# Four weight units behind three FFNs multiply the unnormalised sum and are corrected afterwards

## The chip, the cores and the metric

The kernel runs on one core of a Trainium2 chip. The metric is the time of one execution on the device in microseconds; the median of three runs is shown. Engines are named as in the profile: PE is TensorE (matmuls; PEld its weight loads), DVE is VectorE, ACT is ScalarE, POOL is GpSimd, SP issues most transfers.

## What is computed

The input is 256 tokens of 1024 features in fp32. A first block (a conformer convolution module and a convolutional FFN) is followed by a second block of two layers. Each layer is FFN, mixer, FFN, and a layer norm ends each of the three:

```python
for i in range(2):
    x = layer_norm(ALPHA * x + 0.5 * swiglu(x, gate1[i], up1[i], down1[i]), ln_g[i, 0], ln_b[i, 0])
    proj = x @ w_in[i]                     # i = 0: RWKV-7 mixer, i = 1: stick-breaking attention
    heads = concat([mix(proj), memory_attention(mq, mem_k, mem_v)])
    x = layer_norm(ALPHA * x + heads @ w_out[i], ln_g[i, 1], ln_b[i, 1])
    x = layer_norm(ALPHA * x + 0.5 * swiglu(x, gate2[i], up2[i], down2[i]), ln_g[i, 2], ln_b[i, 2])
```

`layer_norm(y)` is `(y - mean) / sqrt(var + eps) * g + b` over the features of a token. A product of its result with a weight column w is therefore `r * (g*y @ w) - r*mean * (g @ w) + (b @ w)`, with r the reciprocal deviation of the token.

## The kernel before

Activations lie features on partitions: eight tiles of 128 features by 256 tokens. All products are made of three fp32r products: a weight is split into a rounded high part (ScalarE, L226) and the rest (VectorE, L235), an activation likewise (`xh`, `xl`, together `xx`; `split_act`, L499). Weights come as a stream of units of 128 x 1024; `Stream.take` (L243) hands out the next one and splits four units ahead, `split_hi` and `split_lo` (L218, L229) do one part of one unit. A unit of an up-projection is one tile of 128 outputs: eight blocks (one for each input tile) of three matmuls of 256 columns, or two where the wide form (`mm_wide`, L367) moves high and low part in one matmul of 512 columns.

The program is issued in the order of the Python code; each engine runs its own instructions in that order, and waits by semaphores. So what stands earlier in the code on an engine's queue must be finished before what stands later.

`ffn` (L656): 22 pairs of gate and up tiles (`wide_gate`, L714), four banks of PSUM at a time, then the down-projection, eight output tiles of 22 blocks each. Behind each output tile stand the residual (`on_tile`, L1098), its square on ScalarE and a running sum on GpSimd. The layer norm behind it is `Norm.finish` (L1208): short matmuls against a column of 1/1024 give mean and mean square, `keep_warm` (L339) issues 12 matmuls whose result nobody reads, ScalarE and VectorE make the reciprocal deviation, four transposes broadcast deviation and shift into the bank `bc`, and six more unread matmuls follow. `ln_out` (L546) then scales and shifts the tiles group by group (one, one, two, two, two): two VectorE operations that read `bc`, ScalarE's gain and bias into `xh`, VectorE's gain and bias into `xr`, and VectorE's difference into `xl`.

Next come the first four units: `gemm_wides` (L404) in an FFN, `gemm_outs` (L392) in the mixers, both block by block of the input over all four units, so that block k needs only tile k of `xx`. In the RWKV mixer these four are the inputs of the low-rank projections and the memory queries (`project`, L1437); `shifted` (L1427) mixes a tile with the one of the token before, on ScalarE and then VectorE; two transfers of low-rank weights are issued by ScalarE. In stick-breaking they are the memory queries and the first pair of queries and keys (L1963 to L1968).

From there a planner, `weave` (L1297), interleaves generators while the program is built. Each `yield pe, dve, more` says how much time of TensorE and VectorE a step is taken to need and how much later the task may go on; a task whose time has not come is passed over, and lower priorities go first. It fixes an order once; at run time nothing is reordered. The tasks that matter here:

```python
def lora(self, lora, dwa):        # RWKV, priority 3
    yield 0.0, 0.0, 3.0
    ...                           # products of lora weights with dwa, two per step
def attention(self):              # stick-breaking, priority 1
    yield 0.0, 0.0, 1.2
    ...                           # scores of pair p from queries and keys
```

The main task (priority 5) makes the remaining units through `gemm_out_parts` (L377), which yields 0.66 after every second block.

## Time and profile before

| | us |
|---|---|
| median of three runs (lowest, highest) | 1495.84 (1494.53, 1499.8) |
| the profiled execution | 1493.3 |
| its span | 1491.5 |
| PE busy | 1435.5 (96%) |
| DVE busy | 1064.8 (71%) |
| ACT busy | 843.4 (57%) |
| POOL busy | 109.2 (7%) |

The table's busy times are sums over the span, and matmuls overlap each other in the record: the starts of two neighbours lie closer together than one of them lasts. So the starts are what tells TensorE's pace. Times in the text count from the span's start. The chain of waits follows the work that ended last back from the end; a row of the timeline gives start, duration, engine, line, operation, output and inputs, and in brackets how long the engine had been idle before and what ended that.

### The profile page before, as it was taken

To read this page: it belongs to the slowest core of one execution; us is meant where nothing else is said; L and a number is where in the kernel's file an instruction comes from. 1 tells how busy PE (TensorE), PEld (TensorE's weight loads), DVE (VectorE), ACT (ScalarE), POOL (GpSimd) and SP (SyncE) were. 2 spreads that over 40 slices of the span, in tenths; PEclk is the share of its full clock that TensorE was granted. 3 is DMA by queue.
4 is the path that set the end of the run, shared out by engine and by line. 5 is a ranking of instruction groups with operands and counts; after the bars stand their busy time and mean duration, and the time that the engine had idled before them with its cause. 6 is when DMAs were issued, how large, how long until landed. Compare 5 with 4: busy or idle time off the path is not lost.

```text
span 1491.5 us, 26146 instructions
## 1 busy us (share of the span) xinstructions
PE 1435.5 (96%) x10737; PEld 1288.1 (86%) x10737; DVE 1064.8 (71%) x1677; ACT 843.4 (57%) x1479; POOL 109.2 (7%) x96
## 2 busy tenths in 40 slices
PE   8888899999999999999999999999999999999997
PEld 7868799998888888898888888888888988888886
DVE  7897788884877657888568776587765655687753
ACT  6796466685565536651346655365553566465542
POOL 1110100000000010040010000100001011100010
PEclk9998899999999999999989999999999999999998
DMA  9775445565355553230034555535555322265540
GB/s 381 285 253 187 155 170 194 186 228 198 147 194 196 188 188 125 92 136 4 3 112 176 192 198 185 183 139 200 183 184 198 127 109 103 99 225 195 198 169 29
DMA packets 39145, 250.38 MB, mean 168 GB/s; under 512 B 4337, under 2 KB 4849, under 8 KB 12274
## 3 DMA queue, kind: packets, MB, share of 16 engines
q1 hardware_dynamic: 38594, 247.60, 45.5%
q8 instruction: 84, 1.38, 0.4%
q10 hardware_dynamic: 432, 1.11, 0.2%
q14 instruction: 35, 0.29, 0.1%
HBM read 247.65 MB, written 1.05 MB: 167 GB/s over the span
## 4 chain that ended last, share of the span: by engine, by line
PE 82%; DVE 11%; ACT 5%; issue 2%; POOL 0%; DVEq 0%; ACTq 0%; POOLq 0%
PE acc L370 26%; PE acc L358 15%; PE gu L358 7%; PE gu L370 7%; PE gu L363 4%; PE gu L364 4%; PE r L1737 2%; PE acc L412 2%; DVE wlo L235 2%; PE st L1219 1%; DVE mraw L595 1%; ACT whi L226 1%; PE gu L346 1%; DVE ys L555 1%; PE acc L862 1%
## 5 line engine op out<-in xcount | busy, mean ns | idle before, releaser
L235 DVE TENSOR_TENSOR wlo<-wraw,whi 128x1024 fp32r<-128x1024 f32 x416 | 522.4, 1266 | 42.4 <-ACT whi L226 40.3
L226 ACT CAST whi<-wraw 128x1024 fp32r<-128x1024 f32 x416 | 427.3, 1045 | 27.1 <-PE acc L364 7.4
L370 PE MATMUL acc<-hx,whi 128*128 128x512 f32 x880 | 310.8, 398 | 0.0
L358 PE MATMUL acc<-xx,wlo 128*128 128x256 f32 x1088 | 293.3, 284 | 3.5 <-ACT xx L561 2.2
L370 PE MATMUL acc<-xx,whi 128*128 128x512 f32 x832 | 289.6, 390 | 0.0
L358 PE MATMUL gu<-xx,wlo 128*128 128x256 f32 x992 | 278.3, 281 | 0.0
L358 PE MATMUL acc<-hx,wlo 128*128 128x256 f32 x880 | 247.6, 281 | 0.0
L358 PEld LDWEIGHTS acc<-xx,wlo 128*128 128x128 f32 x1088 | 201.8, 190 | 9.0 <-ACT xx L561 4.7
L370 PEld LDWEIGHTS acc<-hx,whi 128*128 128x128 f32 x880 | 165.4, 188 | 40.5
L358 PEld LDWEIGHTS gu<-xx,wlo 128*128 128x128 f32 x992 | 186.9, 188 | 0.2
L370 PEld LDWEIGHTS acc<-xx,whi 128*128 128x128 f32 x832 | 156.2, 188 | 32.7
L358 PEld LDWEIGHTS acc<-hx,wlo 128*128 128x128 f32 x880 | 166.1, 189 | 0.0
L363 PE MATMUL gu<-xx,whi 128*128 128x256 f32 x544 | 157.7, 290 | 2.3 <-ACT u L747 2.3
L370 PE MATMUL gu<-xx,whi 128*128 128x512 f32 x448 | 156.5, 390 | 0.0
L364 PE MATMUL gu<-xx,whi 128*128 128x256 f32 x544 | 151.9, 279 | 0.0
L1179 ACT ACTIVATE ys<-ys 128x256 f32<-128x256 f32 (+1 forms) x66 | 28.6, 437 | 157.2 <-DVE ys L1102 140.3
L363 PEld LDWEIGHTS gu<-xx,whi 128*128 128x128 f32 x544 | 102.3, 188 | 11.2 <-issue 8.4
L364 PEld LDWEIGHTS gu<-xx,whi 128*128 128x128 f32 x544 | 102.4, 188 | 0.7 <-issue 0.7
L370 PEld LDWEIGHTS gu<-xx,whi 128*128 128x128 f32 x448 | 84.1, 188 | 17.6
L1100 DVE SCALAR_TENSOR_TENSOR ys<-xr,acc 128x256 f32<-128x256 f32 x32 | 13.5, 422 | 95.0 <-PE acc L370 95.0
L722 ACT COPY lows<-acc 128x256 f32<-128x256 f32 x60 | 22.5, 374 | 104.0 <-PE acc L370 103.9
L1196 POOL TENSOR_TENSOR nsum<-ys 128x512 f32<-128x512 f32 (+1 forms) x9 | 13.2, 1468 | 924.0 <-PE acc L370 621.1
(355 smaller groups left out, 2254.9 us busy)
## 6 DMA issues: line engine op xcount, KB each, us to landing
wraw<-in_w SPq DMA_DIRECT2D x208, 1024.0 KB, 4.8
mraw<-in_mod SPq DMA_DIRECT2D x48, 512.0 KB, 5.6
xr<-in_x SPq DMA_DIRECT2D x2, 512.0 KB, 4.1
m<-in_mem SPq DMA_DIRECT2D x1, 1024.0 KB, 8.1
out<-xr SPq DMA_DIRECT2D x3, 256.0 KB, 2.2
cst<-in_consts SPq DMA_DIRECT2D x1, 546.0 KB
lora<-in_lora ACTq DMA_DIRECT2D x1, 384.0 KB, 3.3
lora_g<-in_lora ACTq DMA_DIRECT2D x1, 384.0 KB, 3.8
```

Source lines behind the costliest of these rows:

```text
L226: b.nc.scalar.copy(out=hi, in_=raw)
L235: b.nc.vector.tensor_tensor(out=lo, in0=raw, in1=hi.bitcast(F32), op=ALU.subtract)
L346: self.nc.tensor.matmul(ps[:, 0, :], lhsT=w[0][:, 0:P], rhs=w[0][:, 0:T], start=True, stop=True, skip_group_check=True)
L358: self.nc.tensor.matmul(out, lhsT=wl, rhs=x[:, 0, :], start=start, stop=False, skip_group_check=True)
L363: mm(out, lhsT=wh, rhs=x[:, 0, :], start=start, stop=False, skip_group_check=True)
L364: mm(out, lhsT=wh, rhs=x[:, 1, :], start=False, stop=False, skip_group_check=True)
L370: self.nc.tensor.matmul(bank, lhsT=wh, rhs=x, start=False, stop=stop, skip_group_check=True)
L412: self.nc.tensor.matmul(bank, lhsT=wh[:, c], rhs=x[:, k], start=False, stop=k == KD - 1, skip_group_check=True)
L555: nc.vector.tensor_tensor(out=y, in0=y, in1=bc[:, q:q + 1, :].to_broadcast([P, k1 - k0, T]), op=ALU.add if q else ALU.mult)
L722: nc.scalar.copy(out=lows[:, 1, :], in_=banks[1][:, 1, :])
L1179: b.nc.scalar.activation(out=b.ys[:, k0:k1, 1, :], in_=y, func=AF.Square)
L1737: mm(o[rows[q], i, :], lhsT=lhsT, rhs=rhs, start=True, stop=True, skip_group_check=True)
```

## The change

Behind the FFNs of layer norms 0, 2 and 3 (in front of the RWKV mixer, of the next FFN and of the stick-breaking mixer; not behind the last) `ln_ahead` takes the place of `Norm.finish` and `ln_out`. Under the down-projection each finished tile y is also turned into high and low part of g*y (`raw_operand`), in a tile with two more columns that hold g and b (`raw_gains`). The next four units multiply these 258 columns, in two `gu` banks and two accumulator banks. Six blocks of the first stand before the statistics matmuls, two blocks and three of the second between them and the broadcast, the rest behind it; the unread matmuls are gone there. The broadcast is copied to SBUF (`bcs`). For each unit ScalarE copies its two last columns and makes the shift from them, VectorE scales the 256 columns and adds the shift (`shift`, `scale`, `add`). The normalisation of the tiles themselves stands in between; six of the eight tiles of `xr` are made on GpSimd. Two weight units are split ahead of the first product and two behind the first tile.

The consumers change with it. The FFN starts with two pairs of finished gate and up tiles (`pre_gate`) and runs `gemm_wides` on the next two pairs; the order of its banks is turned. The mixers take the four corrected tiles, in RWKV in `first`, ahead of `project`, and make their next four units block by block, yielding 1.42 after each block (`gemm_outs_parts`); `SB_ORDER` is changed to that. In the remaining norms six unread matmuls stand ahead of the broadcast instead of twelve, and behind the FFNs the seventh tile's sum is made on GpSimd too.

```diff
-SB_ORDER = [("p", 1), ("v", 0), ("p", 2), ("p", 3), ("v", 1), ("p", 4), ("p", 5), ("v", 2)]
+SB_ORDER = [("p", 1), ("p", 2), ("v", 0), ("p", 3), ("v", 1), ("p", 4), ("p", 5), ("v", 2)]
...
-    WARM0 = 12
+    WARM0 = 6
...
+        self.zz = ap.tile([P, KD, 2, T + 2], F32R, name="zz")
+        self.pres = [ap.tile([P, T], F32, name=f"pre{i}") for i in range(4)]
+        self.bcs = ap.tile([P, 2, T], F32, name="bcs")
+        self.shift = [ap.tile([P, T], F32, name=f"shift{i}") for i in range(2)]
+        self.wgb = [ap.tile([P, 2], F32, name=f"wgb{i}") for i in range(4)]
...
-        ws = [self.stream.take() for _ in range(2 * len(banks))]
+        ws = [self.stream.take(ahead) for _ in range(2 * len(banks))]
+        if not ahead:
+            for _ in range(2):
+                self.stream.split_hi()
+            for _ in range(2):
+                self.stream.split_lo()
         for k in range(KD):
             c = slice(k * P, k * P + P)
...
+    def raw_gains(self, li):
+        for i, v in enumerate(self.ln_cols(li)):
+            self.split_act(self.zz[:, :, 0, T + i], self.zz[:, :, 1, T + i], v)
+    def raw_operand(self, k, li):
+        g = self.ln_cols(li)[0][:, k:k + 1]
+        y, zh, zl = self.ys[:, k, 0, :], self.zz[:, k, 0, :T], self.zz[:, k, 1, :T]
+        self.nc.scalar.activation(out=zh, in_=y, func=AF.Copy, scale=g)
+        self.nc.vector.scalar_tensor_tensor(out=zl, in0=y, scalar=g, in1=zh.bitcast(F32), op0=ALU.mult,
+                                            op1=ALU.subtract)
+    def ln_ahead(self, st, eps, li, func, accs):
+        nc = self.nc
+        tt = nc.vector.tensor_tensor
+        g, b = self.ln_cols(li)
+        ws = [self.stream.take(False) for _ in range(4)]
+        banks = [t.rearrange("p a t -> p (a t)")[:, :T + 2]
+                 for t in [self.gu_tile() for _ in range(2)] + [self.acc_tile(i) for i in accs]]
+        pre, bcs = self.pres, self.bcs
+        def unit(i, k0, k1):
+            wh, wl = ws[i]
+            for k in range(k0, k1):
+                c = slice(k * P, k * P + P)
+                self.mm3(banks[i], wh[:, c], wl[:, c], self.zz[:, k], k == 0, k == KD - 1)
+        def shift(i):
+            w, t = self.wgb[i], self.shift[i % 2]
+            nc.scalar.copy(out=w, in_=banks[i][:, T:T + 2])
+            nc.scalar.activation(out=t, in_=bcs[:, 1, :], func=AF.Identity, scale=w[:, 0:1],
+                                 bias=w[:, 1:2])
+        def scale(i):
+            tt(out=pre[i], in0=banks[i][:, :T], in1=bcs[:, 0, :], op=ALU.mult)
+        def add(i):
+            tt(out=pre[i], in0=pre[i], in1=self.shift[i % 2], op=ALU.add)
+        def normal(k0, k1):
+            y = self.ys[:, k0:k1, 0, :]
+            for q in range(2):
+                tt(out=y, in0=y, in1=bcs[:, q:q + 1, :].to_broadcast([P, k1 - k0, T]),
+                   op=ALU.add if q else ALU.mult)
+            for k in range(k0, k1):
+                nc.scalar.activation(out=self.xh[:, k, :], in_=self.ys[:, k, 0, :], func=AF.Identity,
+                                     scale=g[:, k:k + 1], bias=b[:, k:k + 1])
+                (nc.vector if k < 2 else nc.gpsimd).tensor_scalar(
+                    out=self.xr[:, k, :], in0=self.ys[:, k, 0, :], scalar1=g[:, k:k + 1],
+                    scalar2=b[:, k:k + 1], op0=ALU.mult, op1=ALU.add)
+        def low(k0, k1):
+            tt(out=self.xl[:, k0:k1, :], in0=self.xr[:, k0:k1, :],
+               in1=self.xh[:, k0:k1, :].bitcast(F32), op=ALU.subtract)
+        for _ in range(2):
+            self.stream.split_hi()
+        for _ in range(2):
+            self.stream.split_lo()
+        unit(0, 0, 6)
+        parts = st.finish_parts(eps, None)
+        next(parts)
+        unit(0, 6, 8)
+        unit(1, 0, 3)
+        bc = next(parts)
+        unit(1, 3, 8)
+        unit(2, 0, 8)
+        unit(3, 0, 8)
+        nc.scalar.copy(out=bcs, in_=bc)
+        normal(0, 1)
+        shift(0)
+        scale(0)
+        low(0, 1)
+        add(0)
+        for _ in range(2):
+            self.stream.split_hi()
+        for _ in range(2):
+            self.stream.split_lo()
+        if func is not None:
+            self.preload(func)
+        normal(1, 2)
+        shift(1)
+        scale(1)
+        low(1, 2)
+        normal(2, 4)
+        add(1)
+        low(2, 4)
+        normal(4, 6)
+        shift(2)
+        scale(2)
+        add(2)
+        low(4, 6)
+        normal(6, 8)
+        shift(3)
+        scale(3)
+        add(3)
+        low(6, 8)
+        self.pre = pre
...
-            first = [banks(0), banks(1)]
+                return [self.gu_tile() for _ in range(2)] if j % 3 == 0 else [
+                    self.acc_tile(2 * (j % 3) - 2 + o) for o in range(2)]
+            n = 0
+            if self.pre is not None:
+                for n in range(2):
+                    gates.append(self.pre_gate(self.pre[2 * n:2 * n + 2], hs[n][:, 0, :], hs[n][:, 1, :]))
+                    next(gates[-1])
+                n = 2
+                self.pre = None
+            first = [banks(n), banks(n + 1)]
             (self.gemm_outs if conv else self.gemm_wides)(first[0] + first[1], self.xx)
             for j, bk in enumerate(first):
...
                 st.square(o, o + 1)
+                if li is not None:
+                    self.raw_operand(o, li)
...
+        if self.last:
+            self.ln_end(st, 4 * LN_EPS, li, func)
+        else:
+            self.ln_ahead(st, 4 * LN_EPS, li, func, (0, 1) if li == 2 else (0, 2))
...
+            for li in range(6):
+                if li in (1, 4):
                     self.leave_dense()
-                    self.mark(mix)
-                    (StickBreaking if layer else Rwkv)(self).run(3 * layer + 1)
-                if f"ffn{2 + 2 * layer}" in self.parts:
-                    self.swiglu_ln(3 * layer + 2, AF.Silu)
+                    self.mark("mixer")
+                    (StickBreaking if li == 4 else Rwkv)(self).run(li)
+                    continue
+                if li in (0, 2):
+                    self.leave_dense()
+                    self.open_ahead()
+                    self.enter_dense()
+                self.swiglu_ln(li, (AF.Sigmoid, None, AF.Silu, None)[li] if li < 4 else AF.Silu)
...
-            if eng is None or self.n > KD - 2:
+            if eng is None or self.n > KD - self.late:
                 self.rest.append(t)
...
+        b = self.b
+        parts = self.finish_parts(eps, func)
+        next(parts)
+        if ahead:
+            b.stream.split(b.stream.n_use + b.LEAD)
+        b.fill(fill[0], b.WARM0)
+        bc = next(parts)
+        b.fill(fill[1], b.WARM)
+        return bc
...
+        nc, b = self.nc, self.b
         self.omm = self.keep.tile([P, 20], F32, name="omm")
         nc.vector.tensor_scalar(out=self.omm, in0=b.vec("rwkv_mu_2", 0, 20), scalar1=-1.0,
                                 scalar2=1.0, op0=ALU.mult, op1=ALU.add)
+        ys = b.ys.rearrange("p k a t -> p (k a) t")
+        self.sgw, self.aa, self.dwa, self.dg = ys[:, 0:NP], ys[:, NP:2 * NP], ys[:, 12], ys[:, 13]
+        self.mq = ys[:, 14:16]
+        pre, b.pre = b.pre, None
+        self.shifted(self.dwa, pre[0], 18)
+        self.shifted(self.dg, pre[1], 19)
+        for i in range(2):
+            nc.scalar.copy(out=self.mq[:, i, :], in_=pre[2 + i])
+        b.close_ahead()
+    def project(self):
...
+        early = [self.po.tile([P, 2, T], F32, name="early", tag="r") for _ in range(2)]
+        self.early = True
+        yield from b.gemm_outs_parts(early, b.xx)
+        for n, (name, g) in enumerate(RWKV_PAIRS):
             first = RWKV_FIRST[name] + 2 * g
-            gu = b.gu_tile()
             z = self.work(name, [2, T], 3)
-            yield from b.gemm_out_parts(gu[:, 0, :], b.xx)
-            yield 0.66, 0.0, 0.0
-            yield from b.gemm_out_parts(gu[:, 1, :], b.xx)
+            if n < 2:
+                gu = early[n]
+                self.early = n == 0
+            else:
...
-        banks = [self.ps().rearrange("p (a t) -> p a t", a=2), b.gu_tile()]
-        b.gemm_outs(banks, b.xx)
-        nc.scalar.copy(out=self.mq, in_=banks[0])
-        self.queries(0, banks[1])
+        pre, b.pre = b.pre, None
+        for i in range(2):
+            nc.scalar.copy(out=self.mq[:, i, :], in_=pre[i])
+        self.queries(0, pre[2:])
+        b.close_ahead()
         self.add(self.attention(), 1)
         for tl in range(2):
             self.add(self.mem_attention(tl, ys[:, 12 + tl]), SB_MEM)
-        for kind, i in SB_ORDER:
+        early = [b.gu_tile() for _ in range(2)]
+        yield from b.gemm_outs_parts(early, b.xx)
+        for n in range(2):
+            self.queries(n + 1, [early[n][:, i, :] for i in range(2)])
```

## Rows read from the trace of the kernel before

**Rows 1.** chain of the work that ended last, share of the span by engine

```profile
PE 82%; DVE 11%; ACT 5%; issue 2%; POOL 0%; DVEq 0%; ACTq 0%; POOLq 0%
```

**Rows 2.** timeline, first end: start, duration, engine, line, operation [idle before, releaser]

```profile
560.68 0.40 PE L370 MATMUL acc<-hx,whi 128*128 128x512 f32 x1
...
567.29 0.74 PE L400 MATMUL r<-xx,whi 128*128 128x256 f32 x4 [0.96 <-ACT xx L561]
...
579.63 0.28 PE L363 MATMUL gu<-xx,whi 128*128 128x256 f32 x1
...
583.71 0.28 PE L358 MATMUL gu<-xx,wlo 128*128 128x256 f32 x1
```

**Rows 3.** timeline, second and third end, TensorE

```profile
965.80 0.40 PE L370 MATMUL acc<-hx,whi 128*128 128x512 f32 x1
...
986.75 0.28 PE L358 MATMUL gu<-xx,wlo 128*128 128x256 f32 x1
...
1159.63 0.40 PE L370 MATMUL acc<-hx,whi 128*128 128x512 f32 x1
...
1179.76 0.28 PE L363 MATMUL gu<-xx,whi 128*128 128x256 f32 x1
...
1182.74 0.71 PE L2061 MATMUL z<-q,k 64*128 64x256 f32 x4 [0.72 <-ACT k L1999]
```

**Rows 4.** timeline, the norm behind the first end

```profile
562.04 0.42 ACT L1179 ACTIVATE ys<-ys 128x256 f32<-128x256 f32 x1 [5.47 <-DVE ys L1102]
...
562.63 1.03 PE L1219 MATMUL st<-inv,ys 128*128 128x1 f32 x8
...
565.73 0.88 DVE L555 TENSOR_TENSOR ys<-ys,bc 128x256 f32<-128x256 f32 x2 [0.76 <-PE bc L1246]
...
576.33 0.69 DVE L573 TENSOR_TENSOR xx<-xr,xx 128x512 fp32r<-128x512 f32 x1 [0.39 <-ACT xx L561]
```

**Rows 5.** groups by line and shape: busy us, mean ns, idle before

```profile
L235 DVE TENSOR_TENSOR wlo<-wraw,whi 128x1024 fp32r<-128x1024 f32 x416 | 522.4, 1266 | 42.4 <-ACT whi L226 40.3 <-PE acc L358 2.0
...
L226 ACT CAST whi<-wraw 128x1024 fp32r<-128x1024 f32 x416 | 427.3, 1045 | 27.1 <-PE acc L364 7.4 <-PE acc L370 6.0 <-PE acc L412 5.1
...
L561 ACT ACTIVATE xx<-ys,vecs 128x256 fp32r<-128x256 f32 x40 | 22.4, 596 | 34.2 <-DVE ys L555 34.2
...
L555 DVE TENSOR_TENSOR ys<-ys,bc 128x512 f32<-128x512 f32 x36 | 24.3, 680 | 1.2 <-PE bc L1246 1.1
...
L1196 POOL TENSOR_TENSOR nsum<-nsum,ys 128x256 f32<-128x256 f32 x10 | 9.1, 905 | 28.8 <-ACT ys L1179 28.4
...
L1844 POOL COPY Z<-cst 128x512 f32<-128x512 f32 x3 | 1.7, 611 | 0.0
```

**Rows 6.** the lora transfer (last column: us to landing), its product, a table load

```profile
lora<-in_lora ACTq DMA_DIRECT2D x1, 384.0 KB, 3.3
...
583.91 1.13 PE L1503 MATMUL r<-ys,lora 64*128 64x256 f32 x4
...
1176.44 1.28 ACT L328 ACT_TABLE_LOAD   x1
```

**Rows 7.** stretches: length, PE PEld DVE ACT POOL busy, PEclk, DMA, GB/s

```profile
1190.00:1200.00 10.00, 10.00 (x70) 8.57 (x70) 5.65 (x9) 7.17 (x15) 1.02 (x3) 1.00 0.27 107
...
115.00:119.40 4.40, 1.24 (x13) 1.01 (x9) 3.77 (x9) 1.75 (x4) 0.00 (x0) 0.90 0.55 164
...
119.40:122.80 3.40, 3.40 (x17) 3.40 (x17) 3.40 (x4) 2.39 (x5) 0.00 (x0) 0.50 0.04 14
```

**Rows 8.** timeline, the norm behind the RWKV mixer

```profile
776.05 0.16 DVE L1243 SCALAR_TENSOR_TENSOR rn<-st,rn 128x2 f32<-128x2 f32 x1
...
777.47 1.06 PE L1246 MATMUL bc<-head,rn 128*128 128x128 f32 x4
```

**Rows 9.** timeline, GpSimd and VectorE side by side

```profile
1281.23 3.33 POOL L1196 TENSOR_TENSOR nsum<-nsum,ys 128x512 f32<-128x512 f32 x2 [0.26 <-ACT ys L1179]
...
1283.33 1.78 DVE L1196 TENSOR_TENSOR nsum<-ys 128x512 f32<-128x512 f32 x1
```

More of the change, by code (lines that the diff above doesn't have):

```diff
@@ L709, in ffn @@
                 st.square(o, o + 1)
+                if li is not None:
+                    self.raw_operand(o, li)
                 st.sum(o, o + 1, "pool")
@@ L725, in wide_gate, with pre_gate @@
         nc.vector.tensor_tensor(out=u, in0=banks[1][:, 0, :], in1=lows[:, 1, :], op=ALU.add)
+        nc.vector.tensor_tensor(out=u, in0=u, in1=g, op=ALU.mult)
+        nc.scalar.copy(out=hh, in_=u)
+        yield
+        nc.vector.tensor_tensor(out=hl, in0=u, in1=hh.bitcast(F32), op=ALU.subtract)
+    def pre_gate(self, pre, hh, hl):
+        nc = self.nc
+        g, u = pre
+        nc.scalar.activation(out=g, in_=g, func=AF.Silu)
+        yield
         nc.vector.tensor_tensor(out=u, in0=u, in1=g, op=ALU.mult)
@@ L1167, with __init__ @@
 class Norm:
[L1170 to L1171 removed]
+    def __init__(self, b, mean, late=2):
+        self.b, self.mean, self.late, self.n = b, mean, late, 0
         self.q = 0 if mean else 1
@@ L1221, in finish @@
                     fresh = False
-        if ahead:
-            b.stream.split(b.stream.n_use + b.LEAD)
-        b.fill(fill[0], b.WARM0)
+        yield
         sd = b.tmp.tile([P, 2], F32, name="sd", tag="sd")
@@ L1397, in ps @@
         self.n_ps += 1
-        return (self.pr, self.po)[self.n_ps % 2].tile([P, 512], F32, name="r", tag="r")
+        return (self.pr, self.po)[0 if self.early else self.n_ps % 2].tile(
+            [P, 512], F32, name="r", tag="r")
     def run(self, li):
         b = self.b
-        self.n_ps = 0
+        self.n_ps, self.early = 0, False
         self.ready, self.grams = {}, set()
         with b.pool("keep") as self.keep:
+            self.first()
             with ExitStack() as self.psum:
@@ L1449, in project @@
         nc.scalar.dma_start(out=self.lora_g, in_=b.dr["lora"][:, 768:])
-        self.sgw, self.aa, dwa, self.dg = ys[:, 0:NP], ys[:, NP:2 * NP], ys[:, 12], ys[:, 13]
-        self.mq = ys[:, 14:16]
-        banks = [self.ps().rearrange("p (a t) -> p a t", a=2) for _ in range(2)]
-        b.gemm_outs(banks, b.xx)
-        self.shifted(dwa, banks[0][:, 0, :], 18)
-        self.shifted(self.dg, banks[0][:, 1, :], 19)
-        nc.scalar.copy(out=self.mq, in_=banks[1])
         nc.scalar.activation(out=dwa[:HD], in_=dwa[:HD], func=AF.Tanh)
@@ L1990, in pair @@
         yield from b.gemm_out_parts(gu[:, 1, :], b.xx)
-        self.queries(p, gu)
+        self.queries(p, [gu[:, i, :] for i in range(2)])
         yield 0.66, 0.0, 0.0
@@ L1997, in queries @@
         k = mp.tile([P, T], F32, name="k", bufs=3)
-        nc.scalar.mul(out=q, in_=gu[:, 0, :], mul=0.125)
-        nc.scalar.copy(out=k, in_=gu[:, 1, :])
+        nc.scalar.mul(out=q, in_=gu[0], mul=0.125)
+        nc.scalar.copy(out=k, in_=gu[1])
         self.qk[p] = (q, k)
```

56 lines of the change are left out of this document (31 added, 25 removed).

## The prediction

> **What bounds the kernel now.** I read the chain of work that ended last first: TensorE carries 82% of it [rows 1]. So the question at each place is whether TensorE's stream gets a gap or loses one. Then I went through the timeline at the three ends of FFN that the change touches. The last down-projection matmul starts at 560.68, the first matmul of the next stage at 567.29, and four weight units later the stream goes on at 579.63 [rows 2]. Four units are 96 matmuls; behind them stand 36, whose starts run from 579.63 to 583.71, 0.1166 us apart [rows 2], so four units need 11.2 us. The stretch from 561.08 to 579.63 is 18.55 us long: 7.35 us are lost. The same sum gives 20.55 and 19.73 us, and losses of 9.35 and 8.5 us, at the second and third end [rows 3]. Together 25 us, 1.7% of the span: that is all the change can win there. The cause is the normalisation: statistics, broadcast (readable at 565.73), then VectorE and ScalarE until the last low part begins at 576.33 [rows 4].
>
> **The change, part by part.** Positions below are on the first end's clock, where the last down matmul ends at 561.08; the other two ends lie 405.12 and 598.95 us later [rows 2, 3].
>
> *Four units go ahead.* Operand tiles 0 to 6 are made in the down-projection, under its matmuls. TensorE runs 18 matmuls (2.1 us, to 563.2), then 16 short statistics matmuls. Eight take 0.9 to 1.03 us [rows 4], so they end at 565.0. Fifteen more matmuls end at 566.75. Meanwhile ScalarE squares the last tile (562.46 [rows 4]), makes its operand (0.6) and splits two weight units (2.0 [rows 5]), to 565.0; VectorE makes their low parts to 566.45, and only then the deviation, since its queue is in order. From the last statistics matmul to a readable broadcast takes 2.1 us now [rows 4]; with that queueing I put it at 568.1. TensorE waits 0.7 us of this and ends the remaining 63 matmuls at 575.45. So four units are done 4.2 us earlier than now at the first end. That is the visible gain.
>
> *The normalisation behind it gets longer.* This is the step that decides, because the same two queues now also hold four corrections and two more weight splits. From rows: a 256-column VectorE operation 0.35 us start to start and 0.88 for two that depend [rows 4]; two dependent 512-column ones 1.4 (0.68 each [rows 5]) and a low part 0.6 to 0.69 [rows 4]; ScalarE 0.6 for one high part and 1.1 for two [rows 5]; a correction on ScalarE (two columns, then one scaled tile) 0.75, an estimate from the 0.6. Copy of the broadcast to SBUF 568.75. Tile 0: normalise 569.7, high part 570.35, low 570.75, shift 571.1, add 571.5. Two splits: ScalarE 573.1, VectorE 574.5. Tile 1: normalise 575.4, low 576.5. Tiles 2 and 3: normalise 577.9, high parts 579.0, low 579.6. Tiles 4 and 5: normalise 581.0, high 582.1, shift 582.9, add 583.3, low 583.9. Tiles 6 and 7 the same way: 585.3, 586.4, 587.2, 587.6 and 588.2. So the input of the next stage is complete at 588.2, where it is at 577.0 now [rows 4]. A pair of tiles costs 4.3 us, since the add waits for ScalarE and the low part stands behind it.
> Bounds: VectorE's own work without any wait is 14.7 us, so not before 583.5. The GpSimd operations that take over six of the eight residual tiles have no like in the trace: a one-input copy of 512 columns takes 0.61 us and a two-input add of 256 columns 0.905 [rows 5]. At the first price ScalarE's high parts are later anyway; at the second each pair gains 0.8 us, and the end is about 590. I take the copy's, the nearer in kind.
>
> *Second end (FFN to FFN).* Eight units end at 592.8 now (986.75 [rows 3] and four units more). Afterwards the four wide units trail the pairs: the low part of tile 6 at 588.2, then two products of 1.4 us less the part already done, 590.5. Gain 2 us (0 to 6 between the bounds).
>
> *First end (FFN to RWKV).* The first lora product stands in TensorE's queue behind block 3 of the eight that the new four units have, because the planner's clock adds 1.42 per block and lora asks for 3.0 after the first. Its operands come from a correction's result, and both the token shift and the issue of the lora transfer stand on ScalarE behind the whole normalisation; the token shift's scalars are made on VectorE behind the last low part. So: scalars 588.4, transfer issued by 589.2, landing 3.3 us later [rows 6], 592.5. TensorE finished block 3 at 582.0 and waits 10.5 us. Now this product starts at 583.91 [rows 6] with 5.5 units done [rows 2]; then it starts at 592.5 with 6 done, the difference worth 1.4 us. Loss 592.5 - 583.9 - 1.4 = 7.2 us; 2.5 at the early bound, 9 at the late.
>
> *Third end (FFN to stick-breaking).* The first scores stand behind block 1 and need the corrected queries and keys. ScalarE does, after the last shift (587.2), a table load of 1.28 [rows 6], two copies, queries, keys: 590.0. Now scores start at 1182.74, 583.8 here [rows 3], with 4.75 units done (six of eight blocks of the fifth) against 5 then, worth 0.7: loss 590.0 - 583.8 - 0.7 = 5.5 us (0.8 to 7.3). Nothing gives it back: TensorE is busy 10.00 of 10 us in the stage behind [rows 7], and the changed order of units fills no more than before.
>
> *The clock.* In the stretch 115.0 to 119.4 TensorE was busy 1.24 of 4.4 us, and the next 3.4 us were granted 0.50, the lower level [rows 7]. A wait of 10 us should do the same; matmuls cost double there, and I add 1.7 us at the first and third end (0 to 3 each). The Trainium skill (TensorE: Matmul & The Clock Gate, HAM oscillation) says likewise that waits in the stream make TensorE start again at the lower clock; that speaks against the change, and the rows agree.
>
> *Half the warm-up matmuls* before a broadcast, six for twelve: the reciprocal was ready at 776.2 and the transposes began at 777.47 [rows 8], 1.25 us lost, and six matmuls fewer remove it. Four norms keep this path; I take 2.5 us in all (0 to 5). The seventh tile's statistics on GpSimd instead of TensorE lie in the wait for the last square: nothing.
>
> Sum: 7.2 + 1.7 + 5.5 + 1.7 - 2 - 2.5 = 11.6 us. The profiled execution took 1493.3 us, 1.8 more than its span; 1504.9 on its level. The runs shown have their median 2.5 us higher, so I predict 1507.4, rounded to 1507.
>
> **The rivals.** *Faster: the gain stays whole.* If the corrected tiles reach the mixers before TensorE has used up the four units behind, which is about 581 to 582 on this clock, the waits vanish and each end keeps 4 to 6 us: 3 x 5 + 2.5, about 1478. For it: the loss of 24 us is real, and ScalarE is idle for much of these stretches. Against: VectorE's floor of 583.5 lies behind that point. Chance 0.20, for queues that overlap better than their rows.
> *No change.* VectorE at its floor, 583.5: losses 2.5 + 0.8 + 2 for the clock, gains 4 + 2.5, near 1495. Chance 0.14.
> *The port.* A VectorE sum with two SBUF inputs took 1.78 us, where 0.69 is usual for its size [rows 4], and ended after GpSimd's two sums of 3.33 us [rows 9]. The broadcast now sits in SBUF, so all scaling has two SBUF inputs, next to six GpSimd operations at each end. If each such pair costs another 0.8 us, the sum rises by 2.4 at each mixer and the gain at the second end goes: about 1515. The Trainium skill (GPSIMD Engine Reference, Key points) says GpSimd shares its SBUF interfaces with VectorE and contends with instructions that have two SBUF inputs; by that rule this rival is the case, and rows 9 agree with it. Chance 0.12.
>
> **How the numbers follow.** Forecast 0.54 (1500.5 to 1513), port 0.12, no change 0.14, faster 0.20. About 0.3%, 4.5 us, is what a measurement of this kernel can tell from no change. Slower 0.66, same 0.14, faster 0.20. The range runs from 1486, which leaves out half of the faster case, to 1517, past the port's price.
>
> **What would show it.** Right: at the first end TensorE idle for about 10 us in front of the first lora product, released by the lora transfer or the tanh; at the third a like gap in front of the scores, released by the keys' copy; the last low part 27 us behind the last down matmul; the second end a little shorter; granted clock near 0.5 behind both gaps. Wrong: if the four units don't start right behind the down-projection; if the last low part comes before 582; if lora and scores come later in TensorE's queue than I read from the planner's yields; or if a bank of the units isn't free for the products behind.

## The result, and the profile after

| | us |
|---|---|
| kernel before, median (lowest, highest) | 1496.5 (1494.5, 1499.8) |
| changed kernel, median (lowest, highest) | 1513.8 (1511.0, 1515.5) |
| ratio, 95% interval | 1.0112 (1.0086 to 1.0137) |
| span of the profiled execution, before and after | 1491.5 and 1509.0 |

The change makes the kernel 1.1% slower. The forecast was 1507, with a range of 1486 to 1517; the measured 1513.8 lies just above the 1500.5 to 1513 that it gave to its own case. The span grew by 17.5 us, and a table by stage tells where. A stage runs from the end of the last down-projection matmul to the next such mark (for a mixer, to the first statistics matmul behind it, and the FFN from there on).

| stage, us | before | after | difference |
|---|---|---|---|
| start to the end of the convolution FFN | 368.5 | 369.8 | +1.3 |
| FFN 1 | 192.6 | 191.9 | -0.7 |
| first end and RWKV | 209.7 | 224.9 | +15.1 |
| FFN 2 | 195.4 | 194.5 | -0.9 |
| second end and FFN 3 | 193.8 | 190.5 | -3.3 |
| third end and stick-breaking | 124.2 | 130.0 | +5.9 |
| FFN 4 | 193.3 | 194.2 | +0.9 |
| tail | 14.0 | 13.2 | -0.7 |

The first row is no effect of the change: over all profiled executions below, that mark lies between 367.3 and 370.5 us.

TensorE at the first end and in the RWKV stage behind it, the lines that answer to [rows 2, 6] (start, duration, engine, line, operation, and in brackets the idle time before it and what ended that):

```profile
561.26 0.40 PE L384 MATMUL acc<-hx,whi 128*128 128x512 f32 x1
561.50 0.28 PE L377 MATMUL gu<-zz,whi 128*128 128x258 f32 x1
...
591.28 2.04 PE L1683 MATMUL r<-ys,lora 64*128 64x256 f32 x4 [9.96 <-DMA lora<-in_lora]
612.58 1.05 PE L1747 MATMUL r<-cst,sqk 128*128 128x2 f32 x8 [1.10 <-ACT sqk L1742]
623.42 1.27 PE L1747 MATMUL r<-cst,sqk 128*128 128x2 f32 x8 [1.29 <-ACT sqk L1742]
636.69 1.08 PE L1539 MATMUL r<-mpt,memv 128*64 128x256 f32 x4 [2.69 <-ACT mpt L1534]
```

The four units start right behind the down-projection, at 561.50, and run through to 575.38 without a wait: the old loss of 7 us is gone. Then TensorE stands still for 9.96 us in front of the first lora product, and three waits of 1.1 to 2.7 us follow: for `sqk` (the squares of the keys) and `mpt` (transposed weights of the memory attention). The trace of before has no wait of 0.45 us or more from 568 to 670 us.

The third end, to set against [rows 3]:

```profile
1198.99 1.23 PE L2246 MATMUL z<-q,k 64*128 64x256 f32 x4 [10.80 <-ACT k L2184]
```

The scores wait 10.80 us for the keys' copy, where they waited 0.72.

The normalisation behind the first end, VectorE and ScalarE, for [rows 4]:

```profile
568.55 0.88 DVE L572 TENSOR_TENSOR ys<-ys,bcs 128x256 f32<-128x256 f32 x2 [1.36 <-ACT bcs L598]
...
582.63 0.68 DVE L582 TENSOR_TENSOR xx<-xr,xx 128x512 fp32r<-128x512 f32 x1
...
585.85 0.42 DVE L564 TENSOR_TENSOR pre<-acc,bcs 128x256 f32<-128x256 f32 x1 [1.20 <-ACT wgb L559]
586.48 0.42 DVE L567 TENSOR_TENSOR pre<-pre,shift 128x256 f32<-128x256 f32 x1 [0.21 <-ACT shift L560]
586.82 0.68 DVE L582 TENSOR_TENSOR xx<-xr,xx 128x512 fp32r<-128x512 f32 x1
587.42 0.17 DVE L1608 TENSOR_SCALAR omm<-vecs 128x20 f32<-128x20 f32 x1
...
587.78 0.38 ACTq L1627 DMA_DIRECT2D lora<-in_lora  x1
```

The last low part ends at 587.50, 25.8 us behind the last down matmul; before it was 15.9 [rows 2, 4]. The two low parts shown lie 4.19 us apart, the price of a pair; VectorE waits 1.20 us for ScalarE in it. The lora transfer is issued only behind all of this.

The clock (length, busy time of PE, PEld, DVE, ACT, POOL, granted clock, DMA share, GB/s), for [rows 7]:

```profile
585.00:590.00 5.00, 0.00 (x0) 0.00 (x0) 3.31 (x8) 3.73 (x11) 0.84 (x2) 0.50 0.22 42
590.00:595.00 5.00, 3.72 (x12) 2.91 (x13) 2.92 (x4) 2.65 (x4) 0.00 (x0) 0.50 0.64 220
595.00:600.00 5.00, 5.00 (x19) 3.94 (x19) 0.00 (x0) 0.95 (x2) 0.00 (x0) 0.50 0.27 108
600.00:605.00 5.00, 5.00 (x26) 3.83 (x25) 0.00 (x0) 1.30 (x3) 0.00 (x0) 0.85 0.00 0
...
1199.00:1203.00 4.00, 4.00 (x22) 3.62 (x23) 1.23 (x1) 3.94 (x7) 0.00 (x0) 0.60 0.17 33
```

Behind the first end TensorE works at the lower level (0.50) from the first lora product to about 602 us, and once more from 625.4 to 628.8, behind two of the later waits; behind the third end only for some 3 us.

The whole stretch from the last down matmul to the end of RWKV's project stage (up to the wait in front of the `D` products) in one row each, first of the kernel before, then of the changed one:

```profile
561.08:670.74 109.66, 107.23 (x865) 95.01 (x863) 87.86 (x170) 68.67 (x140) 20.64 (x31) 1.00 0.32 114
```

```profile
561.66:687.09 125.43, 109.32 (x839) 96.59 (x837) 88.30 (x173) 72.21 (x151) 24.71 (x37) 0.92 0.29 105
```

The project stage alone grew by 15.8 us, RWKV as a whole by 15.1. This stretch is used below to compare kernels (named as in the headings of the experiments): its length is waits (length less PE busy), plus what the lower clock cost (busy time times one less the granted clock, summed over slices of 3 us), plus work.

| project stage, us | length | waits | lower clock | work |
|---|---|---|---|---|
| before | 109.7 | 2.4 | 0.0 | 107.2 |
| after | 125.4 | 16.1 | 6.8 | 102.5 |
| clock_kept | 122.5 | 7.5 | 1.4 | 113.5 |
| tiles_first | 121.3 | 14.5 | 4.0 | 102.8 |
| behind_blocks | 127.6 | 9.8 | 13.5 | 104.2 |
| tiles_first_behind | 116.2 | 8.3 | 3.0 | 104.9 |
| lora_early | 123.4 | 9.2 | 11.4 | 102.8 |
| pair_by_pair | 131.2 | 10.2 | 17.8 | 103.2 |

The work column shows the gain of the change, 4.7 us at this end. The two columns before it show what was paid: 13.7 and 6.8 us.

Each row is one execution. The part of RWKV behind this stage took 99.4 to 105.3 us in them, and that need be no effect of the first end: `second_and_third`, whose first end and RWKV mixer are as in the kernel before, took 104.2 there. First the kernel before, then that one:

```profile
670.74:770.81 100.07, 92.27 (x1631) 84.60 (x1631) 69.75 (x151) 32.27 (x67) 7.08 (x6) 0.98 0.10 33
```

```profile
670.03:774.26 104.23, 96.41 (x1631) 87.11 (x1632) 69.78 (x151) 32.41 (x67) 7.07 (x6) 0.93 0.09 32
```

The number of matmuls is the same and the granted clock lower, 0.93 for 0.98. So the time of RWKV as a whole can't tell kernels apart that differ by 5 us; the project stage tells more.

### The profile page after: what moved, and what is told of

Its sections match the earlier page's. It is cut to its first block, busy times and chain, and to the rows that moved or that the text cites. A ratio compares the mean times of both kernels' runs of the same rounds, so it can differ in the third digit from the quotient of the medians.

```text
span 1509.0 us, 26075 instructions
## 1 busy us (share of the span) xinstructions
PE 1426.1 (95%) x10652; PEld 1281.6 (85%) x10652; DVE 1079.7 (72%) x1709; ACT 862.4 (57%) x1534; POOL 122.6 (8%) x119
## 3 DMA queue, kind: packets, MB, share of 16 engines
HBM read 247.65 MB, written 1.05 MB: 165 GB/s over the span
## 4 chain that ended last, share of the span: by engine, by line
PE 48%; DVE 4%; ACT 1%; issue 1%; POOL 0%; DVEq 0%; POOLq 0%
PE acc L384 17%; PE acc L372 10%; PE gu L384 5%; PE gu L372 3%; PE r L1917 2%; DVE ys L572 1%; PE gu L377 1%; PE acc L377 1%; PE acc L378 1%; PE st L1387 1%; PE gu L423 1%; PE gu L378 1%; DVE ys L685 1%; PE gu L436 0%; DVE wlo L235 0%
## 5 line engine op out<-in xcount | busy, mean ns | idle before, releaser
L235 DVE TENSOR_TENSOR wlo<-wraw,whi 128x1024 fp32r<-128x1024 f32 x416 | 507.7, 1236 | 34.7 <-ACT whi L226 29.0
L384 PE MATMUL acc<-xx,whi 128*128 128x512 f32 x816 | 284.1, 390 | 0.0
L372 PE MATMUL acc<-xx,wlo 128*128 128x256 f32 x1008 | 280.3, 283 | 0.0
L372 PE MATMUL gu<-xx,wlo 128*128 128x256 f32 x976 | 271.3, 283 | 1.6 <-ACT xx L630 1.0
L372 PEld LDWEIGHTS acc<-xx,wlo 128*128 128x128 f32 x1008 | 190.5, 191 | 0.8
L384 PE MATMUL gu<-xx,whi 128*128 128x512 f32 x432 | 150.9, 390 | 0.0
L377 PE MATMUL gu<-xx,whi 128*128 128x256 f32 x480 | 140.4, 292 | 2.4 <-ACT u L899 2.4
L378 PE MATMUL gu<-xx,whi 128*128 128x256 f32 x480 | 135.5, 282 | 0.0
L377 PEld LDWEIGHTS gu<-xx,whi 128*128 128x128 f32 x480 | 91.7, 191 | 9.1 <-issue 6.2
L384 PEld LDWEIGHTS gu<-xx,whi 128*128 128x128 f32 x432 | 81.1, 188 | 17.0
L378 PEld LDWEIGHTS gu<-xx,whi 128*128 128x128 f32 x480 | 91.9, 191 | 0.7 <-issue 0.7
L725 DVE TENSOR_TENSOR mraw<-mraw,cact 128x1024 f32<-128x1024 f32 x48 | 60.6, 1272 | 0.4 <-DMA mraw<-in_mod 0.4
```

Of the source, the lines that this page charges most:

```text
L235: b.nc.vector.tensor_tensor(out=lo, in0=raw, in1=hi.bitcast(F32), op=ALU.subtract)
L372: self.nc.tensor.matmul(out, lhsT=wl, rhs=x[:, 0, :], start=start, stop=False, skip_group_check=True)
L377: mm(out, lhsT=wh, rhs=x[:, 0, :], start=start, stop=False, skip_group_check=True)
L378: mm(out, lhsT=wh, rhs=x[:, 1, :], start=False, stop=False, skip_group_check=True)
L384: self.nc.tensor.matmul(bank, lhsT=wh, rhs=x, start=False, stop=stop, skip_group_check=True)
L725: self.nc.vector.tensor_tensor(out=raw, in0=raw, in1=self.cact, op=ALU.mult)
```

## The experiments

Theory: the change gains at each end what the old norm left idle, and loses more in front of the mixers, because lora and scores stand early in TensorE's queue while their inputs stand at the end of a longer normalisation. Rivals: the length of that normalisation alone, the clock alone, the port between GpSimd and VectorE. Each ratio is to the kernel before, timed on the same chip.

**The second end alone (second_end).** In the loop, only layer norm 2 goes through `ln_ahead`; mixers and the other norms as before.

```diff
-            if li in (0, 2):
+            if li == 2:
...
-        if self.last:
+        if li != 2:
             self.ln_end(st, 4 * LN_EPS, li, func)
```

> The change is made at the second end alone (FFN to FFN); both mixers, their first units and the other norms stay as in the kernel before, with twelve unread matmuls. Theory: an FFN takes the corrected tiles without asking for them early, so the second end keeps its gain: from the last down matmul to the end of eight units 28.3 us against 31.8 in the kernel before, and 3 to 4 us off the whole time, about 1493 against 1496.5. Rival: the end looks shorter in the changed kernel only because the stage in front of it was disturbed, or the gain is given back in the FFN behind: within 1 us of the kernel before.

1491.98 us, ratio 0.9982 (0.9970 to 0.9994). The stage took 190.6 us against 193.8, as in the changed kernel. The part with no early consumer keeps its gain.

**Six unread matmuls for twelve, alone (warm0_alone).** `WARM0 = 6` in the kernel before.

> The kernel before, with six unread matmuls in front of every broadcast instead of twelve and nothing else. Theory of the prediction: seven norms behind FFNs and mixers lose about 0.6 us each at full clock, 2 to 4 us in all, about 1493. Rival: the unread matmuls keep the clock up, and where it falls the transposes and what follows run at half speed: no gain, or up to 2 us slower, 1496 to 1499.

1490.31 us, ratio 0.9974 (0.9959 to 0.9989): 3.9 us faster. That is for seven norms, 0.56 us each; the prediction's 2.5 us are for the four that keep this path in the changed kernel, 0.63 each. FFN 2 and FFN 3 gained 1.8 and 1.7 us. FFN 4 lost 0.5, as the changed kernel lost 0.9 there. At its start, behind the stick-breaking mixer, the four transposes ran at full speed before and at the lower level, as those of [rows 8], in the changed kernel. First the kernel before, then the changed one:

```profile
1289.28 0.60 PE L1246 MATMUL bc<-head,rn 128*128 128x128 f32 x4
```

```profile
1307.05 1.06 PE L1412 MATMUL bc<-head,rn 128*128 128x128 f32 x4
```

That six matmuls are too few there is not shown: in second_end, with twelve, these transposes ran at the lower level as well, and FFN 4 took 195.9 us.

**Lora and scores behind the eight blocks (behind_blocks).**

```diff
     def lora(self, lora, dwa):
-        yield 0.0, 0.0, 3.0
+        yield 0.0, 0.0, 14.0
...
     def attention(self):
-        yield 0.0, 0.0, 1.2
+        yield 0.0, 0.0, 11.0
```

> The changed kernel, but lora may start 14.0 instead of 3.0 after the planner's start and the scores 11.0 instead of 1.2, so both stand in TensorE's queue behind all eight blocks of the next four units. Theory (the order in TensorE's queue is the cause): both waits of 10 us and the half clock behind them vanish, and with them the later gaps in RWKV; each end then gains what the four units ahead gained: at least 12.7 us of queueing and 5 of clock come back, 1490 to 1497. Rival (the longer normalisation is the cause whatever the order): TensorE waits as long at the blocks that need the last tiles of the input, 1508 to 1514.

1502.20 us, ratio 1.0058 (1.0036 to 1.0081): between the two. The third end behaves as the theory says: stick-breaking 124.8 us against 130.0, and the wait of 10.8 us became two of 1.0 at the last blocks and one of 1.9. RWKV does not, in the profiled execution: 227.8 against 224.9. Its wait of 10 us is gone too, but the clock went in its place:

```profile
583.92 1.21 PE L423 MATMUL early<-xx,whi 128*128 128x256 f32 x8 [1.03 <-DVE xx L582]
588.12 1.20 PE L423 MATMUL early<-xx,whi 128*128 128x256 f32 x8 [1.03 <-DVE xx L582]
594.12 1.27 PE L1747 MATMUL r<-cst,sqk 128*128 128x2 f32 x8 [1.06 <-ACT sqk L1742]
```

```profile
585.00:590.00 5.00, 3.97 (x34) 3.74 (x33) 2.94 (x9) 3.50 (x10) 1.10 (x2) 1.00 0.10 14
590.00:595.00 5.00, 3.44 (x27) 2.96 (x26) 3.07 (x4) 4.29 (x9) 0.00 (x0) 1.00 0.62 215
595.00:600.00 5.00, 5.00 (x23) 3.94 (x23) 4.33 (x6) 4.45 (x7) 0.00 (x0) 0.61 0.48 157
600.00:605.00 5.00, 5.00 (x16) 3.71 (x16) 1.24 (x3) 1.57 (x4) 0.00 (x0) 0.50 0.87 357
```

No wait at the first end is longer than 1.06 us, but TensorE was busy only 7.4 of 10 us up to 595; then the granted clock fell to 0.50 and stayed there to 620. That execution took 1507.71 us, where the six lie between 1497.99 and 1508.41. By the two ratios the whole time came down by 8 us, 3 more than the third end gives, so in the others RWKV seems to have lost less; no trace of one shows it.

**Unread matmuls in the place of the two waits (clock_kept).** 84 of them ahead of the first lora product and ahead of the first scores.

> The changed kernel with 84 unread matmuls (9.8 us at 0.117 us each) in TensorE's queue in front of the first lora product and as many in front of the first scores, in the place of the two waits. Theory: the first products start when they did, but at the upper clock: 4 to 6 us come back in RWKV and 1.5 to 2 in stick-breaking, 1506 to 1508 against 1513.8. Rival: the slow stretch behind the first wait is the lora products' own (late inputs, fp32 with 64 rows): no change, 1513 to 1515.

1515.08 us, ratio 1.0147 (1.0129 to 1.0165). At the first end the edit does what it says: lora starts at the same distance (29.7 us behind the last down matmul, 29.6 in the changed kernel), and the clock is 1.00 to 630 us:

```profile
578.89 10.22 PE L1681 MATMUL r<-whi 128*128 128x256 f32 x84
589.04 1.13 PE L1688 MATMUL r<-ys,lora 64*128 64x256 f32 x4
...
590.00:595.00 5.00, 5.00 (x32) 4.18 (x32) 1.28 (x2) 1.59 (x4) 0.00 (x0) 1.00 0.60 210
595.00:600.00 5.00, 5.00 (x33) 4.01 (x33) 0.00 (x0) 1.81 (x4) 0.00 (x0) 1.00 0.00 0
```

The project stage came down by 3.0 us, not by the 5.4 that the clock column fell, and RWKV as a whole by 1.2: the later waits grew from 5.6 to 7.0 us, and the work column by 1.0 more than the wait that the 84 matmuls filled. So the lower clock is a part of the 15.8 us only, and the later waits stand without it. At the third end the edit failed: the unread matmuls wrote a bank that the corrections still read, waited 7.98 us for it and then ran in front of the scores, and stick-breaking took 138.2 us. The whole time says nothing about the clock for that reason.

**Tiles ahead of the last corrections (tiles_first).** The order in `ln_ahead`, nothing else:

```diff
         add(1)
-        low(2, 4)
         normal(4, 6)
-        shift(2)
-        scale(2)
-        add(2)
-        low(4, 6)
+        low(2, 4)
         normal(6, 8)
...
+        low(4, 6)
         low(6, 8)
+        for i in (2, 3):
+            shift(i)
+            scale(i)
+            add(i)
```

> The changed kernel with one edit: in the normalisation behind the four units, each pair's scaling stands on VectorE ahead of the low part of the pair before, and the corrections of units 3 and 4 stand behind all tiles. Theory (VectorE waits for ScalarE inside each pair, which makes the chain long): the last low part, 25.2 us behind the last down matmul now, comes at 21 to 22; the second end loses its two waits of 1.1 us; lora and scores start about 1 us earlier, since they stand behind the corrections: 1508 to 1511. Rival (the chain is as long whatever the order, since the engines are full): 1513 to 1515.

1506.94 us, ratio 1.0081 (1.0068 to 1.0095). The last low part starts 21.9 us behind the last down matmul (25.2 before the edit), the second end gained 1.8 us more, lora and scores waited 7.41 and 8.78 us. So a good part of the chain was waiting of VectorE for ScalarE. The time fell by more than forecast, and the trace does not say why: the project stage came down by 4.1 us, 2.8 of them clock, but RWKV as a whole took 226.6 us against 224.9, since the part behind it lost 8.0 us to the clock instead of 1.4.

**No GpSimd (no_gpsimd).** All eight `xr` tiles on VectorE.

> The changed kernel with all eight residual tiles on VectorE instead of six on GpSimd. The port rival: VectorE's sums with two SBUF inputs get shorter without GpSimd beside them, and the time falls by 2.4 us at each mixer in spite of six more operations of 0.35 us on VectorE: about 1510. Theory: they don't get shorter, VectorE has 2.1 us more to do in each chain and loses its 1.0 us wait: 1513.8 to 1517.

1513.34 us, ratio 1.0126 (1.0112 to 1.0141): no difference. VectorE's scaling with two SBUF inputs, grouped over 560 to 590 us, first of the changed kernel, then of this one:

```profile
L572 DVE TENSOR_TENSOR ys<-ys,bcs 128x512 f32<-128x512 f32 x6 | 4.1, 688 | 0.1
```

```profile
L572 DVE TENSOR_TENSOR ys<-ys,bcs 128x512 f32<-128x512 f32 x6 | 4.1, 689 | 0.1
```

688 and 689 ns, and 680 with the broadcast in PSUM [rows 5]. The port costs nothing in the changed kernel. It can, though: with tiles first, GpSimd and VectorE do run at once, and both get slower:

```profile
576.98 4.20 POOL L577 TENSOR_SCALAR xr<-ys,vecs 128x256 f32<-128x256 f32 x4 [20.46 <-DVE ys L572]
...
579.80 1.93 DVE L572 TENSOR_TENSOR ys<-ys,bcs 128x512 f32<-128x512 f32 x2
```

1.05 us for one GpSimd tile where the changed kernel has 0.55 to 0.6, and 1.93 us for two scalings instead of 1.41. The Trainium skill (GPSIMD Engine Reference, Key points) says that GpSimd shares its SBUF interfaces with VectorE and contends with VectorE instructions that have two SBUF inputs; these rows agree. In the changed kernel VectorE stood idle for most of the time that GpSimd worked, for 1.20 us in each of the last two pairs (released by ScalarE) and 1.00 in the one before (released by GpSimd).

**Both orders (tiles_first_behind).** Tiles first, and lora and scores behind the blocks.

> The same edit, and lora and scores behind the eight blocks as well (14.0 and 11.0 in the planner). Theory: with the input complete 3 to 4 us sooner TensorE waits less than 1 us in all at the blocks of the first end, so the clock stays at the upper level there (it was at the lower one from 597 to 620 us with the late order alone, worth 11 us); RWKV comes down by 10 to 15 us against the late order alone, whole time 1485 to 1492. Rival (what is lost in RWKV is lost in the chain from lora to its consumers, whatever the clock): 1497 to 1501.

Median 1501.9 us, ratio 1.0032 (1.0010 to 1.0054); the twelve times spread from 1492.2 to 1506.9, the profiled execution took 1495.7. In that one the clock held at 1.00 to 625 us, and the project stage took 116.2 us, the shortest of the kernels with a changed first end, yet 6.5 more than before: five waits of 0.7 to 1.9 us stand in front of `sqk`, `mpt` and `mex`, 5.8 us more waiting in all, and 3.0 us of clock. Stick-breaking took 122.8 us, below the 124.2 of before: there the theory holds. The twelve times go with the clock: the five below 1496 us have a mean granted clock of 0.974 to 0.978 over their span, the seven above 1501 us one of 0.964 to 0.972. Where in the kernel the difference lies no trace shows. The forecast of 1485 to 1492 was missed.

**Lora's inputs early (lora_early).** With tiles first and late scores; lora keeps its early place, its weights are loaded from the end of the down-projection on, and token shift and tanh stand behind the first corrected tile.

```diff
+        if li == 0:
+            nc.scalar.dma_start(out=self.lora, in_=self.dr["lora"][:, :768])
...
+        if li == 0:
+            dwa = self.ys[:, 6, 1, :]
+            nc.scalar.activation(out=dwa, in_=pre[0], func=AF.Copy, scale=self.omm[:, 18:19])
+            nc.vector.scalar_tensor_tensor(out=dwa[:, 1:], in0=pre[0][:, :T - 1],
+                                           scalar=self.vec("rwkv_mu_2", 18), in1=dwa[:, 1:],
+                                           op0=ALU.mult, op1=ALU.add)
```

> The changed kernel with tiles ahead of the last corrections and the scores behind the eight blocks; lora keeps its early place in TensorE's queue, but its inputs are made early: the transfer of its weights is issued right behind the down-projection, and the token shift and tanh of the first corrected tile stand behind that tile's correction instead of behind the whole normalisation. Theory (at the first end TensorE waited for the lora inputs, and the lower clock and the later waits follow from that): lora starts at 581 to 583 us without a wait over 1 us, the clock stays at the upper level, RWKV takes 207 to 212 us (209.7 in the kernel before, 224.9 in the changed one), whole time 1482 to 1488. Rival (RWKV loses through what ScalarE and VectorE have to do behind the longer normalisation, wherever lora stands): RWKV 216 us or more, 1490 to 1502.

1498.99 us, ratio 1.0030 (1.0016 to 1.0045). Lora starts 23.7 us behind the last down matmul, about as in the kernel before (22.8), and RWKV still takes 227.7 us, 104.3 of it behind the project stage. The rival has the better of it: the early lora inputs alone give nothing back, for of the 8 us that the whole is below tiles_first, 7.0 are stick-breaking's with its late scores (122.3 for 129.3 us). In the project stage waits are 9.2 us, the lower clock costs 11.4:

```profile
582.67 1.49 PE L1694 MATMUL r<-ys,lora 64*128 64x256 f32 x4
...
604.63 1.05 PE L1758 MATMUL r<-cst,sqk 128*128 128x2 f32 x8 [1.09 <-ACT sqk L1753]
...
630.56 1.97 PE L1555 MATMUL r<-mpt,memv 128*64 128x256 f32 x4 [2.87 <-ACT mpt L1550]
```

**One pair after the other (pair_by_pair).** In the last kernel VectorE sat idle for 11.4 us in front of the first token shift of keys, because two pairs of tiles ended together. This makes them in turn, with lora behind the first.

```diff
-        yield from b.gemm_outs_parts(early, b.xx)
         for n, (name, g) in enumerate(RWKV_PAIRS):
...
             if n < 2:
                 gu = early[n]
+                yield from b.gemm_outs_parts([gu], b.xx)
```

> The kernel with lora's inputs made early and one edit more: the two pairs of tiles behind the four units ahead (first keys, first r) are made one after the other, eight blocks each, as in the kernel before, and not together block by block; lora starts behind the first pair (7.0 in the planner). Theory (RWKV loses because both pairs end only with the last of the blocks: VectorE sat idle for 11.4 us in front of the first token shift, and then token shifts, squares and weight splits of two pairs pile up): the first shift of keys starts about 26 us behind the last down matmul (41 with the pairs together, 27 in the kernel before), RWKV 219 us or less against 227.7, whole time 1488 to 1492. Rival (the lower clock alone does it, and any stream with waits there falls to it): RWKV 224 us or more, 1496 to 1501.

1509.16 us, ratio 1.0098 (1.0079 to 1.0118): a miss, and slower. The keys' shift came early, about 28.5 us behind the last down matmul, but the waits came to 10.2 us and the clock cost 17.8, with TensorE at the lower level from 593.2 to 617.1 us, in lora products and what follows them. That late pairs are the cause is not borne out.

**Short waits filled (lora_early_filled).** The kernel with early lora inputs, with 11, 11 and 13 unread matmuls in its three short waits at the first end.

> The kernel with lora's inputs made early and one edit more: 11, 11 and 13 unread matmuls (4.1 us) in the three places where TensorE waited for 1.1 to 1.6 us behind the four units (ahead of blocks 3 and 4 and of the fourth lora product). Without them 11.4 us were lost to the lower clock between the last down matmul and the end of the project stage, and 9.3 us to waits. Theory (three short waits bring the clock down, and in this stream it comes back late): the clock stays at the upper level up to the first token shift, 6 to 11 us come back, RWKV 217 to 222 us against 227.7, whole time 1488 to 1493 against 1499. Rival (the lower clock belongs to the lora products and their neighbours, filled or not): RWKV 225 us or more, 1497 to 1501.

1507.90 us, ratio 1.0077 (1.0058 to 1.0096), and no answer: once more the unread matmuls got a bank that the last corrections were reading, a wait of 8.82 us:

```profile
587.31 2.71 PE L1692 MATMUL junk<-whi 128*128 128x256 f32 x11 [8.82 <-DVE pre L564]
```

**What is worth keeping (second_and_warm0, second_and_third).** The second end with tiles first, `WARM0 = 6`, and both mixers as before; then the same with the third end too, scores behind the blocks.

> The change at the second end alone, with six unread matmuls for twelve in every norm and the tiles ahead of the last corrections. Theory (the gains add): 2.6 for the second end, 4.2 for the matmuls, 1 to 2 for the order: 1486 to 1489 against 1494.5 to 1496.5 of the kernel before. Rival (the clock falls at norms where both come together): 1490 to 1493.

> The change at the second and third end alone, with tiles ahead of the last corrections, scores behind the eight blocks and six unread matmuls; the RWKV mixer and the end in front of it as in the kernel before. Theory: once the scores stand behind the blocks the third end gains a little too, 1 to 3 us beside the same kernel without it: 1482 to 1485. Rival: the waits at the last blocks take all of it, 1485 to 1488.

1485.26 us, ratio 0.9940 (0.9928 to 0.9953), and 1486.22 us, ratio 0.9936 (0.9911 to 0.9960). Both beat both kernels, by 0.6% the one before; between them nothing can be told, and the second lies in its rival's range. In the trace the third end gained 1.2 us (122.8 against 124.0). The project stage of the second kernel took 110.2 us, against 109.7 before and 125.4 after: what this stage loses belongs to the changed first end and to nothing else in the change.

## Why the prediction was right, and where its sizes were off

The sign and the mechanism were right at all three ends; the size at the first was too small. Positions are on the first end's clock of before, as in the prediction.

- **The waits.** Forecast: lora waits 10.5 us and starts at 592.5, the scores start at 590.0, a pair costs 4.3, the last low part ends at 588.2. Measured: 9.96 us, 590.7, 588.6, 4.19 and 586.9. The three positions came 1.3 to 1.8 us early; the forecast's wait of 0.7 us inside the four units did not come. That the order in TensorE's queue causes the wait was shown at the third end (behind_blocks, tiles_first_behind). At the first end moving lora removed the wait and, in the profiled execution, not the loss.
- **The clock at the first end**, forecast 1.7 us, range 0 to 3. It cost 6.8: 5.1 from the first lora product to 601.5 us, 1.7 in the second fall. This term was mis-sized most, by 5.1 us. I took 3.4 us at the lower level from [rows 7] as the length of a stretch everywhere. But 3.4 us is only the length of the window that I read; in the same trace the lower level went on to 132.2 us:

```profile
122.80:132.20 9.40, 8.64 (x38) 8.18 (x39) 5.92 (x14) 4.91 (x9) 0.00 (x0) 0.50 0.56 219
```

With 12.0 us of TensorE's work in the two windows, the row read to its end gives 6.0 us. Behind the first end of behind_blocks and pair_by_pair TensorE stayed at the lower level for 24 us. At the third end 1.7 was about right (clock 0.60 over 4 us).

- **What follows in RWKV**, not in the sum. Waits behind the one for lora, most of them in front of `sqk` and `mpt`, add 5.6 us. I said that nothing gives the loss back, and did not ask whether it breeds more. What makes these waits is open. They need neither the wait for lora (5.1 us in lora_early, where lora starts without a wait) nor the clock (7.0 in clock_kept). A wait of 1.9 to 3.5 us for `mpt` stands in all nine kernels with the changed first end; in the other five no wait for `mpt` reaches 0.5 us. Set against the forecast's 10.5 us of waiting, 1.7 of clock and 3.3 gained, which make 8.9, the project stage shows 13.7, 6.8 and 4.7, which make 15.8.
- **The third end**, forecast +7.2, measured +5.9. **The second**, forecast -2, measured -3.3; a residual wait of 1.1 us before each of two pairs (released by the low part) remained as forecast.
- **The unread matmuls**, forecast -2.5. Alone they gave -3.9 in seven norms, 2.2 for four; in the changed kernel FFN 1, 2 and 4 and the tail show about -1.4 (-0.7, -0.9, +0.9 and -0.7, each from one execution). FFN 1 came down as much in second_end, with twelve (191.8 us), so this sum is rough.
- **The rivals.** Faster and no change are out: VectorE's chain was far from its floor of 583.5. The edit that brought it near (last low part at 583.7) still left the mixers waiting. The port is out for this order, though its time of 1515 came nearest; the reason was another.

The sum of the misses (+6.2 at the first end, +1.1 for the matmuls, -1.3 and -1.3 at the other two) is 4.7 us; the other 1.3 us of the span's growth beyond the 11.6 forecast is the first 368 us, which differ that much between executions. That the misses of either sign offset each other in part is luck.

**Still open:** which arrangement behind the first end would keep the 4.7 us of gained work in RWKV, and what makes the later waits there. Late lora, early lora inputs and pairs in turn each moved waits into clock or back. The two tests meant to separate the lower clock from the waits were spoiled in part or whole by a busy bank.

## What to carry over

Starting products before the normalisation is worth what the next consumer in TensorE's order lets through: follow each early consumer's inputs to the end of the queues on which they now stand, and move the consumer or the inputs in the same edit; here that was enough at the third end, and not at the first. Where TensorE's stream had no waits, several short ones can cost as much as one long one, because the clock goes with them; price the clock by a row read to the end of its stretch, and by more than one such stretch. An unread matmul needs a bank that nobody reads, or it is itself the wait.

## What was not expected of the hardware

- How long TensorE worked at the lower level differed from place to place: some 3 us behind the third end, 10 us from the first lora product of the changed kernel, 24 us in behind_blocks (596 to 620), where the lora products stand too. TensorE was busy all the while (5.00 of 5 us in the slices shown). Whether the stream that follows makes the difference was not tested. The same products ran at 1.00 throughout where the clock had not fallen before them (before, clock_kept): four of them took 1.13 us there and 2.07 at the lower level.
- A fall did not need a long wait: in behind_blocks TensorE was busy for 7.4 of 10 us, with no single wait over 1.06, before the slices with 0.61 and 0.50.
- GpSimd and VectorE slowed each other where both worked on SBUF tiles: 1.05 for 0.55 us, and 1.93 for 1.41.
